# A place for side work inside each projection of a two-layer decoder trunk, and other costs in its plan

## The chip, the cores and the metric

The kernel runs on one core of a Trainium2 chip. The metric is the device time of one execution in microseconds (us); the kernel before takes 852.53 us (median of three runs, 852.04 to 853.74). PE is the tensor engine (PEld its weight loads), DVE the vector engine, ACT the scalar engine, POOL the GpSimd engine, SP the engine that issues the weight DMAs.

## What is computed

Two layers over 256 tokens of width 1024 in float32. One input projection feeds three branches: sliding-window attention with sinks (8 heads of 64, window 128), a gated short convolution, and block-selected attention (which for 256 tokens is plain causal attention of 8 heads). Gates merge them, an output projection, residual and LayerNorm follow, then a SwiGLU network of hidden width 2816, residual and LayerNorm. Cut to its frame, the reference is:

```python
for l in range(2):
    proj = x @ w_in[l]                       # q,k,v | conv h,b,c | q,k,v | three gates
    y_a = sliding_window_attention(a_q, a_k, a_v, sinks[l])
    y_b = b_b * causal_conv3(b_c * b_h, conv_w[l])
    y_c = causal_attention(c_q, c_k, c_v)    # ALiBi, as in y_a
    mix = (sigmoid(g_a) * (y_a @ w_a) + sigmoid(g_b) * (y_b @ w_b) + sigmoid(g_c) * (y_c @ w_c)) @ w_out[l]
    x = layer_norm(ALPHA * x + mix)
    x = layer_norm(ALPHA * x + (silu(x @ w_gate) * (x @ w_up)) @ w_down)
```

## The kernel before

Every large product is computed as three float32r products: a tensor is split into a high part (a copy into float32r) and a low part (the difference), and high x high, high x low and low x high are added in PSUM. Weights come in pieces of 128 x 2048 (139 of them after the first), each loaded by SP as a megabyte. ACT copies the high parts of a piece (`wh`, L180) and DVE subtracts the low parts (`wl`, L181), in two chunks of 1024 columns each. The activations (`xx`, both parts) stay in SBUF.

The main stream of PE is `whole` (L371): it takes one piece and makes two accumulators `acc` of 128 x 256, each from 8 depth steps of three matmuls (`trio`), so 24 matmuls an accumulator. `half_pair` (tile `hp`), `branch` (`br`), `merge` (`gc`) and `project` (`pr`) are the same for other shapes.

Side work of PE is attention, one pair of heads a round, 8 rounds a layer (4 of the sliding window, then 4 of the other, called MoBA in the code): `scores` (tile `s`, 6 matmuls), a softmax on DVE and ACT (tile `prob`), `turned` (6 transposes of `prob` into `tp`, which ACT copies to `pt`), and `mixed` (tile `yp`, probabilities times values, which ACT and DVE split into `y`). The transposes of LayerNorm's output (`xtok`) and of `qh` and `gh` are side work too. POOL computes the convolution's taps (L721 to L724, five products and sums an accumulator); DVE multiplies their sum by an accumulator (L277 `t<-t,acc`) and splits it.

The order on every engine is written when the program is built, by a planner, `Plan`. It keeps a clock of PE (`T.pe`, advanced by `pe_time` for each matmul) and a time at which ACT (A), DVE (V) and POOL (G) are free. A task is a list of operations, each with an engine and a cost. `run` issues, in order of their planned start, all operations that can start before PE's clock; `finish` advances PE's clock to a task's end where PE must wait for it. `dve(n)` and `act(n)` give the cost of an operation on n columns. The function `tick` is where side work gets its place on PE: it runs the planner, and issues a waiting piece only when, by the planned clock, its inputs are there (`settled`), or when it is forced. A tick stands after each accumulator of 24 matmuls. The engines execute their lists in order, with semaphores for the true dependences: if the plan is wrong, the work is still right, but an engine waits.

Of the kernel before, what the change touches and what calls it, by code (L numbers as in the profile page):

```python
# [20 lines left out]
KD = D // P  # L21
# [82 lines left out]
def pe_time(cols):  # L104
    return cols / 2400 + 0.0067


def dve(n):
    return "V", 0.07 + n * 0.00104


def act(n):
    return "A", 0.07 + n * 0.00083


@with_exitstack
def trunk(ctx: ExitStack, tc: tile.TileContext, x, first, w, sinks, conv, ln, out):
# [9 lines left out]
    T = Plan()  # L127
# [88 lines left out]
    def settled(task):  # L216
        return task is None or task.done and task.ready <= T.pe

    def tick(force=False):
        while True:  # L220
            T.run()
            go = [e for e in waiting if force or settled(e[0])]
            if go:
                waiting.remove(go[0])
                if go[0][0] is not None:
                    T.finish(go[0][0])
                go[0][1]()
            elif rounds and not rounds[0].tasks and rounds[0].known(force):
                rounds[0].prepare()
            elif rounds and rounds[0].tasks and not busy[0] and (force or all(settled(t) for t in rounds[0].tasks)):  # L230
                busy[0] += 1
                r = rounds.pop(0)
                T.finish(*r.tasks)
                r.scores()
                if not force:
                    return
            else:
                return
# [3 lines left out]
    def bank(shape, tag, name):  # L242

        t = ps.tile(shape, FT, tag=tag, name=name)
        if len(banks[tag]) >= 4:
            for task in banks[tag].pop(0):
                T.finish(task)
        banks[tag].append([])
        return t, banks[tag][-1]
# [75 lines left out]
    for k in steps:  # L325
        xk_, wk = both[:, k, 0:S], both[:, k, S:].rearrange("p k (m c) -> p m k c", m=2)
        n = (k.stop - k.start) * S
# [38 lines left out]
    def trio(acc, wh, wl, src, first, last):  # L366
        mm(acc, wh, src[:, 0, :], first, False)
        mm(acc, wh, src[:, 1, :], False, False)
        mm(acc, wl, src[:, 0, :], False, last)

    def whole(done, by_step=False):  # L371
        j = take()
        wh, wl = duo(j)
        accs = [bank([P, S], "mm", "acc") for m in range(2)]
        order = [(m, k) for m in range(2) for k in range(KD)]
        if by_step:
            order.sort(key=lambda mk: mk[1])
        for m, k in order:
            acc, users = accs[m]
            trio(acc, wh[:, m, k, :], wl[:, m, k, :], xk[k], k == 0, k == KD - 1)  # L380
            if k == KD - 1:
                if m:
                    drop(j)
                done(m, acc, users)
                tick()
# [36 lines left out]
    def attend(q, k, new_k, xq, xk, v, vsel, far, slopes, sink, dst, when):  # L422
        los = [slice(a * HD, (a + 1) * HD) for a in range(2)]
        pr, pts, tasks = [], [], []

        def soft(a, st, t, s):
            def top():
                nc.vector.tensor_reduce(st[:, 0:1], t[:, 0, :], axis=AX.X, op=OP.max)
                nc.vector.tensor_reduce(st[:, 1:2], t[:, 1:3, :], axis=AX.XY, op=OP.max)
                if sink is not None:  # L430
                    nc.vector.tensor_scalar(st[:, 2:4], st[:, 0:2], sink[1][a], -0.125, op0=OP.max, op1=OP.mult)
                else:
                    nc.vector.tensor_scalar_mul(st[:, 2:4], st[:, 0:2], -0.125)  # L433

            def power():
                nc.scalar.activation(t[:, 0, :], t[:, 0, :], AF.Exp, bias=st[:, 2:3], scale=0.125,  # L436
                                     accum_out=st[:, 4:5])
                nc.scalar.activation(t[:, 1:3, :], t[:, 1:3, :], AF.Exp, bias=st[:, 3:4], scale=0.125,
                                     accum_out=st[:, 5:6])
                if sink is not None:  # L440
                    nc.scalar.activation(st[:, 6:8], st[:, 2:4], AF.Exp, bias=sink[0][a], scale=1.0)

            def scale():
                if sink is not None:
                    nc.vector.tensor_add(st[:, 4:6], st[:, 4:6], st[:, 6:8])
                nc.vector.reciprocal(st[:, 6:8], st[:, 4:6])
                nc.vector.tensor_scalar_mul(t[:, 0, :], t[:, 0, :], st[:, 6:7])
                nc.vector.tensor_scalar_mul(t[:, 1:3, :], t[:, 1:3, :], st[:, 7:8])

            return [  # L450
                dve(384) + (lambda: nc.vector.scalar_tensor_tensor(t, far, -8.0 * slopes[a], s[:, 0:3, :],  # L451
                                                                   op0=OP.mult, op1=OP.add),),
                dve(P) + (lambda: nc.vector.tensor_add(t[:, 0, :], t[:, 0, :], s[:, 3, :]),),
                ("V", 0.75, top), ("A", 1.1, power), ("V", 0.9, scale)]

        def scores():
            ss = [bank([P, 4, P], "o", "s") for a in range(2)]
            for a in range(2):
                s = ss[a][0]
                mm(s[:, 1:3, :], xq[:, a, P:S], xk[:, a, 0, :], True, False)  # L460
                mm(s[:, 1:3, :], xq[:, a, P:S], xk[:, a, 1, :], False, True)
                mm(s[:, 0::3, :], xq[:, a, 0:P], xk[:, a, :, 0:P], True, True)
            for a in range(2):
                st = work.tile([P, 8], FT, name="st", bufs=4)
                pr.append(work.tile([P, 3, P], FT, tag="prob", name="prob", bufs=4))
                tasks.append(after(ss[a][1], soft(a, st, pr[a], ss[a][0])))
            later(tasks[-1], turned)

        def turned():
            T.finish(*tasks)  # L470
            for a in range(2):
                tp, users = turn(lambda i: pr[a][:, i, :], 3)
                pts.append(work.tile([P, 3, P], FT, name="pt"))
                tasks.append(after(users, copy(pts[a], tp, 384)))
            later(tasks[-1], mixed)

        def mixed():
            T.finish(*tasks)
            yp, users = bank([P, S], "o", "yp")
            for a in range(2):  # L480
                nc.tensor.matmul(yp[los[a], :], v[:, 0, vsel[a]], pts[a][:, 0:2, :], start=True, stop=False)  # L481
            for a in range(2):
                nc.tensor.matmul(yp[los[a], P:S], v[:, 1, vsel[a]], pts[a][:, 2, :], start=False, stop=True)
            T.pe += pe_time(4 * 384)
            at["y"].append(after(users, halve(dst, yp, S), due=8.0))
            busy[0] -= 1

        rounds.append(Round(when, q, k, new_k, xq, xk, scores))
# [450 lines left out]
```

## Time and profile before

| | |
|---|---|
| median of 3 runs | 852.53 us (852.04 to 853.74) |
| profiled execution: time, span | 849.59 us, 847.8 us |
| PE busy | 831.9 us, 98% |
| DVE busy | 583.0 us, 69% |
| ACT busy | 455.1 us, 54% |
| POOL busy | 51.8 us, 6% |
| mean granted TensorE clock | 0.998 |

A busy time is the union of an engine's instructions. Matmuls overlap in their pipeline: one of 128 x 256 is shown with some 280 ns, while the next starts some 115 ns later. So PE's rate is read from starts, and its loss from gaps and from starts that come late. An engine's idle time is put down to the instruction that ended it (the releaser).

### The profile page before, as it was taken

How to read it: one execution, taken by the hardware profiler on the slowest of the kernel's cores; microseconds unless marked ns; L12 is line 12 of the kernel's file. 1: busy time of each engine (PE TensorE's matmuls, PEld its weight loads, DVE VectorE, ACT ScalarE, POOL GpSimd, SP SyncE). 2: the span in 40 equal slices, each digit the busy share in tenths (PEclk: the TensorE clock that was granted, in tenths of full speed). 3: DMA queues.
4: the chain of work that ended last, by engine and by line, in shares of the span. 5: the costliest groups of instructions: out<-in, count | busy, mean ns of one | idle time of the engine just before them, and what ended most of it. 6: DMA issues, size and time to landing. Idle time of an engine off the chain costs nothing.

```text
span 847.8 us, 15535 instructions
## 1 busy us (share of the span) xinstructions
PE 831.9 (98%) x6388; PEld 791.2 (93%) x6388; DVE 583.0 (69%) x978; ACT 455.1 (54%) x809; POOL 51.8 (6%) x81
## 2 busy tenths in 40 slices
PE   8999999999999999999999999999999999999996
PEld 7989989999899999988899899999998999999885
DVE  5678888677967566545657898886688566566435
ACT  6767587746525445434347857786573345444320
POOL 2003400000100000000000034000000000000000
PEclk9999999999999999999999999999999999999999
DMA  9753525555655555556337352545657365555511
GB/s 316 282 211 137 199 101 198 164 186 199 248 199 200 181 172 194 199 191 235 121 106 255 138 197 101 177 150 174 226 188 281 124 225 195 196 171 183 197 50 49
DMA packets 23462, 155.15 MB, mean 183 GB/s; under 512 B 2624, under 2 KB 2912, under 8 KB 5984
## 3 DMA queue, kind: packets, MB, share of 16 engines
q1 hardware_dynamic: 21888, 149.17, 50.1%
q0 software_dynamic: 1216, 4.22, 1.5%
q8 instruction: 50, 0.82, 0.4%
q10 hardware_dynamic: 288, 0.79, 0.3%
q14 instruction: 20, 0.16, 0.1%
HBM read 153.11 MB, written 1.05 MB: 182 GB/s over the span
## 4 chain that ended last, share of the span: by engine, by line
PE 83%; DVE 6%; ACT 4%; DMA 3%; POOL 2%; issue 1%; SPq 0%; POOLq 0%; DVEq 0%; ACTq 0%
PE acc L252 38%; PE pr L252 18%; PE hp L252 8%; PE br L252 8%; PE gc L252 5%; PE cv L252 3%; DMA raw<-w 2%; PE tp L265 2%; DVE wl L181 1%; ACT wh L180 1%; DMA gb<-ln 1%; PE s L252 1%; PE yp L481 1%; POOL hh L723 1%; DVE prob L451 1%
## 5 line engine op out<-in xcount | busy, mean ns | idle before, releaser
L252 PE MATMUL acc<-xx,wh 128*128 128x256 f32 x2304 | 405.1, 280 | 2.4 <-ACT wh L270 2.4
L181 DVE TENSOR_TENSOR wl<-raw,wh 128x1024 fp32r<-128x1024 f32 x266 | 321.5, 1228 | 116.0 <-ACT wh L180 114.9
L180 ACT ACTIVATE wh<-raw 128x1024 fp32r<-128x1024 f32 x266 | 273.4, 1054 | 185.5 <-PE acc L252 81.9
L252 PEld LDWEIGHTS acc<-xx,wh 128*128 128x128 f32 x2304 | 351.0, 189 | 3.4 <-ACT wh L270 2.9
L252 PE MATMUL acc<-xx,wl 128*128 128x256 f32 x1152 | 321.7, 279 | 0.3 <-DVE wl L271 0.2
L252 PEld LDWEIGHTS acc<-xx,wl 128*128 128x128 f32 x1152 | 216.4, 188 | 0.8 <-DVE wl L271 0.7
L252 PE MATMUL hp<-wh,xx 128*128 128x256 f32 x384 | 70.5, 281 | 0.0
L277 DVE TENSOR_TENSOR g<-g,acc 128x256 f32<-128x256 f32 x72 | 30.0, 416 | 58.7 <-PE acc L252 58.7
L252 PE MATMUL br<-y,wh 128*128 128x256 f32 x384 | 66.7, 278 | 0.0
L252 PE MATMUL pr<-wh,hidA 128*128 128x512 f32 (+1 forms) x216 | 60.7, 366 | 0.0
L252 PEld LDWEIGHTS hp<-wh,xx 128*128 128x128 f32 x384 | 59.5, 188 | 0.0
L252 PEld LDWEIGHTS br<-y,wh 128*128 128x128 f32 x384 | 58.3, 189 | 0.0
L252 PE MATMUL hp<-wl,xx 128*128 128x256 f32 x192 | 53.5, 279 | 0.0
L252 PE MATMUL br<-y,wl 128*128 128x256 f32 x192 | 53.5, 278 | 0.0
L252 PEld LDWEIGHTS pr<-wh,hidA 128*128 128x128 f32 x216 | 39.1, 189 | 6.7
L252 PE MATMUL gc<-xx,wh 128*128 128x256 f32 x256 | 44.5, 278 | 0.0
L252 PE MATMUL pr<-wh,hidB 128*128 128x512 f32 (+1 forms) x144 | 41.8, 366 | 0.0
L252 PE MATMUL pr<-wl,hidA 128*128 128x512 f32 (+1 forms) x108 | 39.6, 366 | 0.0
L252 PEld LDWEIGHTS gc<-xx,wh 128*128 128x128 f32 x256 | 38.9, 189 | 0.0
L436 ACT ACTIVATE prob<-prob,st 128x128 f32<-128x128 f32 x32 | 12.6, 395 | 45.3 <-DVE st L433 23.3
L252 PEld LDWEIGHTS hp<-wl,xx 128*128 128x128 f32 x192 | 36.1, 188 | 0.0
L252 PEld LDWEIGHTS br<-y,wl 128*128 128x128 f32 x192 | 36.0, 188 | 0.0
(133 smaller groups left out, 976.9 us busy)
## 6 DMA issues: line engine op xcount, KB each, us to landing
raw<-w SPq DMA_DIRECT2D x136, 1024.0 KB, 4.9
gb<-ln POOLq DMA_DIRECT2D x8, 512.0 KB, 5.9
raw<-w SPq DMA_DIRECT2D x6, 512.0 KB, 10.4
first<-first SPq DMA_DIRECT2D x2, 512.0 KB, 7.6
xtok<-x SPq DMA_DIRECT2D x2, 512.0 KB, 6.2
out<-xtok SPq DMA_DIRECT2D x3, 256.0 KB, 2.0
first<-first ACTq DMA_DIRECT2D x1, 512.0 KB, 7.7
first<-first ACTq DMA_DIRECT2D x1, 256.0 KB, 4.2
```

The costliest lines, as they stand in the source:

```text
L180: return [act(n) + (lambda: nc.scalar.activation(wh[:, s], raw[j][:, s], AF.Copy),), dve(n) + (lambda: nc.vector.tensor_sub(wl[:, s], raw[ ...
L181: dve(n) + (lambda: nc.vector.tensor_sub(wl[:, s], raw[j][:, s], wh[:, s].bitcast(FT)),)]
L252: nc.tensor.matmul(acc, a, b, start=start, stop=stop)
L265: nc.tensor.transpose(tp[:, i, :], src(i), ident)
L277: return [dve(n) + (lambda: nc.vector.tensor_mul(dst, a, b),)]
L436: nc.scalar.activation(t[:, 0, :], t[:, 0, :], AF.Exp, bias=st[:, 2:3], scale=0.125, accum_out=st[:, 4:5])
L451: dve(384) + (lambda: nc.vector.scalar_tensor_tensor(t, far, -8.0 * slopes[a], s[:, 0:3, :], op0=OP.mult, op1=OP.add),),
L481: nc.tensor.matmul(yp[los[a], :], v[:, 0, vsel[a]], pts[a][:, 0:2, :], start=True, stop=False)
L723: nc.gpsimd.tensor_mul(other, up[:, i, n:S + n], tap[n])
```

## The change

A tick also stands in the middle of each accumulator's 24 matmuls, after 12 (depth step 4 of 8), except where the first piece goes by depth step (`by_step`). And the plan's costs are larger: an operation of n columns on DVE is planned with 0.15 + 0.00106 n us in place of 0.07 + 0.00104 n, on ACT with 0.18 + 0.00085 n in place of 0.07 + 0.00083 n; the three softmax steps with 0.95, 1.5 and 1.1 us in place of 0.75, 1.1 and 0.9; and PE's clock gets 0.1 us more for `scores` and 0.25 us more for `mixed`. No operation is added or taken away: only the order changes.

```diff
 def dve(n):
-    return "V", 0.07 + n * 0.00104
+    return "V", 0.15 + n * 0.00106
 
 
 def act(n):
-    return "A", 0.07 + n * 0.00083
+    return "A", 0.18 + n * 0.00085
...
             trio(acc, wh[:, m, k, :], wl[:, m, k, :], xk[k], k == 0, k == KD - 1)
+            if k == KD // 2 - 1 and not by_step:
+                tick()
             if k == KD - 1:
...
-                ("V", 0.75, top), ("A", 1.1, power), ("V", 0.9, scale)]
+                ("V", 0.95, top), ("A", 1.5, power), ("V", 1.1, scale)]
...
             ss = [bank([P, 4, P], "o", "s") for a in range(2)]
+            T.pe += 0.1
...
-            T.pe += pe_time(4 * 384)
+            T.pe += pe_time(4 * 384) + 0.25
```

What this does to the order is shown at two places. The first is on PE, in the second sliding-window round of layer 0: the last matmuls of an accumulator between the transposes of `prob` and the products `yp`, with the rows of before marked - and those of the changed kernel + (lines 481 and 483 have become 484 and 486).

```order
-L252 MATMUL acc<-xx,wh 128x256 x2
-L252 MATMUL acc<-xx,wl 128x256
-L252 MATMUL acc<-xx,wh 128x256 x2
-L252 MATMUL acc<-xx,wl 128x256
-L252 MATMUL acc<-xx,wh 128x256 x2
-L252 MATMUL acc<-xx,wl 128x256
-L252 MATMUL acc<-xx,wh 128x256 x2
-L252 MATMUL acc<-xx,wl 128x256
-L481 MATMUL yp<-pt,mix 64x256 x2
-L483 MATMUL yp<-pt,mix 64x128 x2
+L484 MATMUL yp<-pt,mix 64x256 x2
+L486 MATMUL yp<-pt,mix 64x128 x2
```

Twelve matmuls leave the space between the transposes and `yp` and come behind the next scores: 12 are left of 24. The same happens in 5 rounds of each layer (the second, third, fifth, seventh and eighth); in the first it was 12 matmuls of twice the width before and is still, in the fourth and sixth it stays 24.

The second place is the fifth round, the first of MoBA, in layer 0. On ACT before, from the softmax's last powers (L436, L438) to the copies `pt`:

```order
L436 ACTIVATE prob,st<-prob,st 128x128
L438 ACTIVATE prob,st<-prob,st 128x256
L270 ACTIVATE y<-t_1223 128x256
L270 ACTIVATE xa<-mix 64x256 x4
L274 ACTIVATE gs<-acc 128x256
L180 ACTIVATE wh<-raw 128x1024
L274 ACTIVATE xa<-mix 64x256 x2
L180 ACTIVATE wh<-raw 128x1024
L274 ACTIVATE pt<-tp 128x384 x2
```

On ACT in the changed kernel, the same stretch (the powers are now L438 and L440):

```order
L438 ACTIVATE prob,st<-prob,st 128x128
L440 ACTIVATE prob,st<-prob,st 128x256
L270 ACTIVATE y<-t_1186 128x256
L274 ACTIVATE xa<-mix 64x256
L180 ACTIVATE wh<-raw 128x1024
L274 ACTIVATE gs<-acc 128x256
L180 ACTIVATE wh<-raw 128x1024
L274 ACTIVATE xa<-mix 64x256
L274 ACTIVATE pt<-tp 128x384
L274 ACTIVATE gs<-acc 128x256
L270 ACTIVATE y<-t_1238 128x256
L274 ACTIVATE pt<-tp 128x384
```

Four of the six `xa` copies (the next round's queries and keys) have gone ahead of the powers, and two other operations now stand between the two `pt` copies. On DVE before, the same round, from the convolution's product `mix<-acc,hh` to the scores' first operation `prob<-far_c,s`; `t_1181` is the sum of taps that POOL makes from that product:

```order
L277 TENSOR_TENSOR mix<-acc,hh 128x256
L181 TENSOR_TENSOR wl<-raw,wh 128x1024
L277 TENSOR_TENSOR mix<-acc,hh 128x256
L181 TENSOR_TENSOR wl<-raw,wh 128x1024 x3
L277 TENSOR_TENSOR t_1181<-t_1181,acc 128x256
L271 TENSOR_TENSOR y<-yp,y 128x256
L271 TENSOR_TENSOR y<-t_1181,y 128x256
L451 SCALAR_TENSOR_TENSOR prob<-far_c,s 128x384 x2
```

On DVE in the changed kernel, where that sum is called `t_1186`:

```order
L181 TENSOR_TENSOR wl<-raw,wh 128x1024 x2
L277 TENSOR_TENSOR mix<-acc,hh 128x256
L181 TENSOR_TENSOR wl<-raw,wh 128x1024
L453 SCALAR_TENSOR_TENSOR prob<-far_c,s 128x384 x2
L455 TENSOR_TENSOR prob<-prob,s 128x128 x2
L430 TENSOR_REDUCE st<-prob 128x1
L431 TENSOR_REDUCE st<-prob 128x1
L435 TENSOR_SCALAR st<-st 128x2
L430 TENSOR_REDUCE st<-prob 128x1
L431 TENSOR_REDUCE st<-prob 128x1
L435 TENSOR_SCALAR st<-st 128x2
L277 TENSOR_TENSOR t_1186<-t_1186,acc 128x256
```

The product with the taps' sum, which stood ahead of the scores' operations, stands behind the maxima of both heads.

## Rows read from the trace of the kernel before

**Rows 1.** The page's first part: busy us, share of the span, instructions.

```profile
PE 831.9 (98%) x6388; PEld 791.2 (93%) x6388; DVE 583.0 (69%) x978; ACT 455.1 (54%) x809; POOL 51.8 (6%) x81
```

**Rows 2.** What PE waited for: us in total, times, longest.

```profile
PE yp L481 <- ACT pt L274: 3.1, 3, 1.5
PE acc L252 <- ACT wh L270: 2.4, 2, 1.5
...
PE tp L265 <- ACT qh L274: 0.8, 1, 0.8
PE tp L265 <- DVE xtok L509: 0.8, 1, 0.8
```

**Rows 3.** Timeline of PE around four visits to yp: start, us, instructions.

```profile
127.20 0.28 PE L252 MATMUL acc<-xx,wl 128*128 128x256 f32 x1
128.21 0.38 PE L252 MATMUL s<-xa 128*128 128x256 f32 x1
...
97.74 0.28 PE L252 MATMUL acc<-xx,wl 128*128 128x256 f32 x1
99.23 0.39 PE L252 MATMUL s<-xa 128*128 128x256 f32 x1
...
111.72 0.28 PE L252 MATMUL acc<-xx,wl 128*128 128x256 f32 x1
114.63 0.38 PE L252 MATMUL s<-xa 128*128 128x256 f32 x1
...
514.88 0.28 PE L252 MATMUL acc<-xx,wl 128*128 128x256 f32 x1
516.50 0.39 PE L252 MATMUL s<-xa 128*128 128x256 f32 x1
```

**Rows 4.** Timeline of ACT in the fifth round of layer 0, idle before in brackets.

```profile
106.03 0.40 ACT L436 ACTIVATE prob<-prob,st 128x128 f32<-128x128 f32 x1 [2.67 <-DVE st L433]
...
108.11 1.45 ACT L270 ACTIVATE xa<-mix 64x256 fp32r<-64x256 f32 x4
...
112.93 0.85 ACT L274 ACTIVATE pt<-tp 128x384 f32<-128x384 f32 x2
```

**Rows 5.** Timelines of POOL and DVE, the same round.

```profile
95.38 1.46 POOL L721 TENSOR_TENSOR t<-mix,cw 128x256 f32<-128x256 f32 x1 [14.87 <-DVE mix L277]
...
101.71 0.74 POOL L724 TENSOR_TENSOR t<-t,hh 128x256 f32<-128x256 f32 x1
102.41 0.61 POOL L721 TENSOR_TENSOR t<-mix,cw 128x256 f32<-128x256 f32 x1
...
96.71 4.45 DVE L181 TENSOR_TENSOR wl<-raw,wh 128x1024 fp32r<-128x1024 f32 x3
102.48 0.42 DVE L277 TENSOR_TENSOR t<-t,acc 128x256 f32<-128x256 f32 x1 [1.32 <-POOL t L724]
```

**Rows 6.** Groups of the page: busy us, mean ns, idle before, releaser.

```profile
L181 DVE TENSOR_TENSOR wl<-raw,wh 128x1024 fp32r<-128x1024 f32 x266 | 321.5, 1228 | 116.0 <-ACT wh L180 114.9
L180 ACT ACTIVATE wh<-raw 128x1024 fp32r<-128x1024 f32 x266 | 273.4, 1054 | 185.5 <-PE acc L252 81.9
```

**Rows 7.** Timelines of PE and DVE at layer 1's first LayerNorm.

```profile
645.25 0.66 PE L265 MATMUL tp<-ident,xtok 128*128 128x128 f32 x4 [0.77 <-DVE xtok L509]
...
644.44 1.41 DVE L509 SCALAR_TENSOR_TENSOR xtok<-xtok,mv,gb 128x512 f32<-128x512 f32 x2 [0.83 <-DMA gb<-ln]
```

**Rows 8.** Timelines of PE and ACT in the seventh round of layer 0.

```profile
137.20 0.82 PE L265 MATMUL tp<-ident,prob 128*128 128x128 f32 x6
140.68 0.65 PE L481 MATMUL yp<-pt,mix 128*64 128x256 f32 x4
...
139.74 0.85 ACT L274 ACTIVATE pt<-tp 128x384 f32<-128x384 f32 x2
```

**Rows 9.** Timelines of PE and ACT behind layer 0's first LayerNorm.

```profile
245.53 1.03 PE L265 MATMUL tp<-ident,xtok 128*128 128x128 f32 x8
...
246.16 1.09 ACT L270 ACTIVATE xx<-tp 128x512 fp32r<-128x512 f32 x2 [2.88 <-PE tp L265]
```

## The prediction

> **What bounds the kernel now.** I read the page's busy times first, then the list of what PE waited for, then PE's timeline at those waits, and last ACT, DVE and POOL at the same times, to see what made PE's input late. PE is busy for 98% of the span [rows 1]. Weights never hold it up behind the start: apart from the 2.4 us at the start for the first copies, every wait of PE in its list is for a small piece of side work [rows 2]. So the change, which takes no matmul away, can win only what PE loses at side work, a few us of 850, and can lose as much by new waits.
>
> How much is lost is read from starts, since a busy PE hides half of it. In an undisturbed round the last matmul ahead of `yp` starts at 127.20 and the next scores at 128.21, 1.01 us later [rows 3]. In the fourth round of layer 0 the same stretch takes 99.23 - 97.74 = 1.49 us, in the fifth 114.63 - 111.72 = 2.91, and in the fourth of layer 1 516.50 - 514.88 = 1.62 [rows 3]. The fifth of layer 1 is taken as equal to that of layer 0 (the three idle gaps sum to 3.1 us with a longest of 1.5 [rows 2], so one more of about 1.5 is there). Lost: 0.48 + 1.90 + 0.61 + 1.90 = 4.9 us.
>
> Why the fifth round: POOL starts the convolution's taps at 95.38 and ends the first sum at 102.45, 7.07 us for five operations; the next accumulator's first tap takes 0.61 us where this one took 1.46 beside DVE's weight subtractions, and these three took 4.45 us [rows 5]. The plan counts 4.0 us for the five. DVE's list has the product with that sum ahead of the scores, and DVE waits 1.32 us there [rows 5]; so the powers start only at 106.03 after ACT had idled 2.67 us, six `xa` copies and two splits follow, and the `pt` copies start at 112.93, when `yp` was due at about 111.8 [rows 3, 4].
>
> **The change, part by part.**
>
> *The costs.* A weight chunk of 1024 was planned with 1.13 us on DVE and 0.92 on ACT, and is now planned with 1.24 and 1.05; the trace has 1.228 and 1.054 [rows 6]. The planned clock of DVE and ACT therefore no longer runs ahead of the engines', while PE's (256 columns: 0.113 us) is still no slower than PE, so a piece that the plan calls settled should mostly be there. What the new list makes of the fifth round: behind the product `mix<-acc,hh` PE has 12 matmuls, 6 transposes, 24 matmuls, `yp` and the scores. At 0.115 us a matmul (3.48 us for the 6 transposes and 24 matmuls of [rows 8]) that is 1.4 + 3.5 + 1.0 + 0.7 = 6.6 us to the scores' end. DVE then runs ten operations, 2 x 0.56 + 2 x 0.29 + 2 x 0.95 = 3.6 us by the plan's new costs, before it comes to the product with the taps' sum, at about 10 us. The taps, started 0.6 us behind the accumulator's end and again beside three subtractions, need 7.1, so they are done at about 7.7 us: DVE doesn't wait, and the powers are ready some 3 us earlier than before. Four `xa` copies have also gone ahead of the powers. I take the fifth rounds' waits as gone, and the fourth's too (24 matmuls remain there, and fewer splits stand ahead): 4.9 us won.
>
> The two `pt` copies of the fifth round are now parted by a `gs` and a `y` copy: 0.48 + 0.38 + 0.42 + 0.48 less 0.3 of overlap is 1.5 to 1.8 us from the first copy's start to the second's end. The transposes allow a first copy about 0.5 us after they start (four of them let the `xx` copy start after 246.16 - 245.53 = 0.63 us [rows 9]), and the second product of `yp` is due 2.4 us after it: a margin of 0.1 to 0.4 us, nothing more.
>
> *The place in the middle.* In 5 rounds of each layer `yp` now stands 12 matmuls nearer to its transposes: 140.68 - 137.20 = 3.48 us becomes 3.48 - 12 x 0.115 = 2.1 us [rows 8]. The copy then has to start within 2.1 - 0.48 = 1.6 us. In the seventh round it started after 139.74 - 137.20 = 2.54 us [rows 8], 0.9 us too late, if ACT's list were as before. In the new list a split and several `xa` copies (1.05 and 0.4 us each) fewer stand ahead of it. Bounds: 0 below, and 0.9 us in the seventh rounds of both layers, with as much in one round more, 2.4 us together; I take 0.5, near the lower end, because each of these lists is shorter by more than 0.9 us.
>
> *LayerNorm.* The first transposes of `xtok` in layer 1 waited 0.77 us [rows 7], for a LayerNorm operation that itself waited 0.83 us for the DMA of `gb` [rows 7]. Both slices now come together 6 matmuls of 512 later, 6 x 0.23 = 1.4 us, which covers the wait: 0.8 won. The other half's second slice goes the other way, in both layers: it comes 24 matmuls later, at the very end of the work that needs only the first half. Behind it stand 2 transposes and the 12 matmuls that read the first slice, about 0.7 + 1.4 + 0.2 = 2.3 us to the first use of the second slice's low part. The copy starts 0.63 us after its transposes, and copy and subtraction take 0.6 + 0.7 us, so it is there after 1.9 to 2.0 us [rows 9]. Cost 0, from 0 to 0.7 us a layer should a split of 1.05 us stand in the way on ACT, which its list doesn't show.
>
> *What stays.* ACT's list is the same as before to the copy that the first `qh` transposes wait for, so that 0.8 us stays, with the start's 2.4 [rows 2]. The weights' loads keep their order on SP, POOL's list too, and the last LayerNorm keeps its order on every engine.
>
> **Sum**, against the profiled execution's own 849.6 us: -4.9 - 0.8 + 0.5 = -5.2, so 844.4. That execution is 2.9 us below the median of the runs, 852.53, and no row shows why; the change is therefore taken from the median: 847.3 us. The likeliest case alone, with its unknown costs (2.4 for 0.5, 1.4 for 0), reaches from 846.8 to 850.6.
>
> **A rule against it.** The trace has a tap of 1.46 us beside weight subtractions and one of 0.61 without [rows 5]. The Trainium skill, page "SBUF — State Buffer", section "Who interferes with whom", says that a DVE instruction with two inputs in SBUF contends with a GpSimd instruction that reads SBUF, by an exclusive lock: the loser is blocked, it doesn't share. By that rule three subtractions of 1.22 us would lengthen five taps of about 3.4 us (0.61 to 0.74 each undisturbed) to 7.1, and the trace's 7.07 agrees. Planned costs taken from the trace can't see this, and the taps' 4.0 is not among the numbers changed; by this rule alone the fifth rounds would keep their waits, which is the first rival.
>
> **Rivals.**
>
> *The taps still decide the fifth rounds.* `yp` stands as far behind its scores as before (96 matmuls, 84 and 12 now, 72 and 24 then). If the product with the taps' sum still holds up DVE, the two waits of 1.9 us come back: a gain of 5.2 - 3.8 = 1.4 us, 851.1 us. For it: the plan's unchanged 4.0 against 7.07, and DVE's wait of 1.32 [rows 5]. Against it: the product stands behind the maxima now, 2 us after the taps should be done. With it I count any case in which the waits only move to other rounds. Chance 0.16.
>
> *The shortened rounds wait: slower.* In ten rounds `yp` needs its copy within 1.6 us of the transposes. If ACT comes as late in all of them as in the seventh of before, each costs 0.9 us: +9.0, with 5.7 won elsewhere, so +3.3, 855.8 us. It turns to a loss when more than six of the ten are that late. For it: the copies of the seventh round, 0.9 us too late by today's list [rows 8]; ACT has 1.05-us splits that can't be interrupted. Against it: the tick only places what the plan calls settled, and ACT idles 185 us ahead of its splits alone [rows 6], so its list has room. Chance 0.10.
>
> **How the numbers follow.** Forecast 0.74, the taps' rival 0.16, the slower one 0.10. A measurement of this kernel can tell about 0.2%, 1.7 us, from no change: the forecast's range lies wholly beyond that on the fast side, the first rival's 1.4 within it, the other's 3.3 beyond it on the slow side. The range of 8 in 10 goes from 845.4 (all 5.7 won, and 1.4 us for runs that spread by 1.7) to 852.4, which takes in the first rival and leaves out the slower one and about as much below.
>
> **What would show it.** Right: PE's waits for `pt` all but gone (3.1 us before), the fifth rounds' stretch from the last matmul to the scores back at about 1.0 us, no wait for `xtok`, the wait for `qh` still there; the powers of the fifth round about 5 us behind their scores. Wrong: a wait of PE for `pt` in the second, third, seventh or eighth rounds, of DVE for POOL's sum ahead of the powers, or of `hp` for `xx` at the second slice. A time above 851 us would say that the planned clock isn't what made PE wait.

## The result, and the profile after

The changed kernel takes 846.41 us (median of four runs, 844.5 to 849.0), the kernel before in the same session 852.28 (851.86 to 853.74): a ratio of 0.9931, 95% interval 0.9912 to 0.995. Forecast were 847.3 us and "faster". Run again beside other kernels, the changed one took 846.91 us (0.9931, 0.9906 to 0.9955) and the one before 852.13. So the gain is 5.2 to 5.9 us.

The first profile of the changed kernel is its slowest run: 849.0 us, span 847.2. What PE waited for in it (us in total, times, longest), to set beside [rows 2]:

```profile
PE acc L252 <- ACT wh L270: 4.5, 2, 3.0
PE spin L322 <- DVE xtok L319: 1.1, 1, 1.1
PE tp L265 <- DVE xtok L512: 0.6, 1, 0.6
...
```

The 3.1 us for `pt` are gone, and so are the 0.8 for `qh`; the wait for `xtok` is nearly as long as it was, and the start has become worse. The start is chance of this execution: the first operands landed late (ACT idled 3.12 us for them), and TensorE's granted clock fell behind PE's 2.98 us wait, as the windows of PE show (the stretch: its length, us busy, instructions, granted clock, DMA share, GB/s; a clock of 0.50 is the lower of its two levels, 1.2 in place of 2.4 GHz, so 0.81 and 0.62 say that PE had it for 3.4 us in all):

```profile
7.00:10.00 3.00, 0.87 (x8) 1.00 0.99 262
10.00:13.00 3.00, 1.93 (x9) 0.81 1.04 422
13.00:16.00 3.00, 3.00 (x19) 0.62 1.02 416
```

The second profile of the same kernel (846.48 us, span 844.7) has the first scores at 44.31 us where the first had 46.54, with the same list of instructions. The account below is therefore made from the second profiles of both kernels (before: 850.74 us, span 849.0).

PE around the fourth and fifth rounds' `yp` of layer 0, in the seventh round, and at layer 1's LayerNorm (first profile of the changed kernel; start, us), which answers to [rows 3, 7, 8]:

```profile
98.66 0.28 PE L252 MATMUL acc<-xx,wl 128*128 128x256 f32 x1
...
99.67 0.98 PE L252 MATMUL s<-xa 128*128 128x256 f32 x6
...
110.03 0.82 PE L265 MATMUL tp<-ident,prob 128*128 128x128 f32 x6
...
111.94 0.28 PE L252 MATMUL acc<-xx,wl 128*128 128x256 f32 x1
112.15 1.09 PE L484 MATMUL yp<-pt,mix 128*64 128x256 f32 x3
...
113.60 0.98 PE L252 MATMUL s<-xa 128*128 128x256 f32 x6
...
135.88 0.82 PE L265 MATMUL tp<-ident,prob 128*128 128x128 f32 x6
138.01 0.65 PE L484 MATMUL yp<-pt,mix 128*64 128x256 f32 x4
...
646.01 1.32 PE L265 MATMUL tp<-ident,xtok 128*128 128x128 f32 x8 [0.59 <-DVE xtok L512]
```

In the fourth round the last matmul now leads to the scores in 1.01 us (1.49 before), in the fifth in 1.66 (2.91 before). The shortened seventh round has `yp` 2.13 us behind its transposes, with no wait. ACT, DVE and POOL in the fifth round, three fences, answer to [rows 4, 5]; the last row of ACT is in the seventh round, the first of DVE in the fourth, the last of DVE at layer 1's LayerNorm:

```profile
104.14 0.40 ACT L438 ACTIVATE prob<-prob,st 128x128 f32<-128x128 f32 x1 [0.44 <-DVE st L435]
...
110.61 0.49 ACT L274 ACTIVATE pt<-tp 128x384 f32<-128x384 f32 x1 [0.85 <-PE tp L265]
111.00 0.38 ACT L274 ACTIVATE gs<-acc 128x256 f32<-128x256 f32 x1
111.96 0.42 ACT L270 ACTIVATE y<-t 128x256 fp32r<-128x256 f32 x1 [0.58 <-DVE t L277]
112.28 0.47 ACT L274 ACTIVATE pt<-tp 128x384 f32<-128x384 f32 x1
...
136.47 0.87 ACT L274 ACTIVATE pt<-tp 128x384 f32<-128x384 f32 x2 [0.28 <-PE tp L265]
```

```profile
88.53 0.42 DVE L277 TENSOR_TENSOR t<-t,acc 128x256 f32<-128x256 f32 x1 [1.31 <-POOL t L727]
...
105.16 0.41 DVE L277 TENSOR_TENSOR t<-t,acc 128x256 f32<-128x256 f32 x1
...
110.04 1.22 DVE L181 TENSOR_TENSOR wl<-raw,wh 128x1024 fp32r<-128x1024 f32 x1
...
111.52 0.41 DVE L277 TENSOR_TENSOR t<-t,acc 128x256 f32<-128x256 f32 x1
...
645.20 1.41 DVE L512 SCALAR_TENSOR_TENSOR xtok<-xtok,mv,gb 128x512 f32<-128x512 f32 x2 [2.02 <-DMA gb<-ln]
```

```profile
97.88 1.46 POOL L724 TENSOR_TENSOR t<-mix,cw 128x256 f32<-128x256 f32 x1 [9.39 <-ACT pt L274]
...
100.97 1.60 POOL L727 TENSOR_TENSOR t<-t,hh 128x256 f32<-128x256 f32 x1
102.65 0.61 POOL L726 TENSOR_TENSOR hh<-mix,cw 128x256 f32<-128x256 f32 x1
103.34 0.74 POOL L727 TENSOR_TENSOR t<-t,hh 128x256 f32<-128x256 f32 x1
```

The taps are done at 104.08 and the product with their sum starts at 105.16 without waiting for them: the powers stand 4.5 us behind the scores instead of 6.8 (106.03 - 99.23 [rows 3, 4]). What is left of the fifth round's wait is the second `pt` copy: behind the `y` copy, which waits 0.58 us for DVE's second product, which stands behind a subtraction of 1.22 us.

DVE's wait for POOL's sum has not gone, it has moved to the fourth round: 1.31 us ahead of the operations on that round's scores (88.53), where it was 1.32 in the fifth [rows 5], and 2.6 us in both layers together before and after. The fourth round's powers start 6.4 us behind its scores, nearly as late as the fifth's did before (6.8). PE loses nothing by it, because `yp` of the fourth round now stands 108 matmuls behind its scores where it stood 96, 12 x 0.113 = 1.36 us more: the copies end 1.1 us before it is due.

Worked out from the starts on PE, the stretches of some kernels, in us, layer 0 and layer 1 (attention: first scores to first `br`; output: from the first `pr` behind merge to the first `hp`; SwiGLU: from there to the next `pr`; the kernels whose first scores come 12 matmuls early have 12 more in attention, and 12 x 0.1133 = 1.36 us are taken off there). The second profiles of both kernels stand first:

| kernel | attention | branch and merge | output, LayerNorm | SwiGLU | span |
|---|---|---|---|---|---|
| before | 112.06, 112.20 | 56.53, 56.53 | 23.25, 23.20 | 126.13, 126.14 | 849.0 |
| changed | 109.94, 109.94 | 56.53, 56.53 | 22.70, 23.45 | 126.00, 126.00 | 844.7 |
| costs alone | 115.22, 115.34 | 54.78, 55.58 | 22.68, 22.97 | 125.95, 125.95 | 852.4 |
| place alone | 111.26, 111.38 | 56.53, 56.53 | 23.44, 23.57 | 126.14, 126.14 | 850.2 |
| copies, gb halves | 111.32, 111.38 | 56.53, 56.53 | 24.25, 24.24 | 126.00, 126.00 | 850.9 |
| place in gates only | 108.96, 108.96 | 56.63, 56.63 | 22.70, 22.70 | 125.95, 125.95 | 843.4 |
| the same, with turns | 108.96, 108.96 | 55.25, 55.25 | 22.67, 22.67 | 122.88, 122.88 | 834.6 |

Before to changed: -2.1 and -2.3 in attention, -0.6 and +0.3 at the LayerNorms, some -0.5 in the rest, and +0.9 up to the first scores (44.74, against 44.31 + 1.36): -4.3, the difference of the spans. The medians' 5.2 to 5.9 are about a microsecond more; what comes before the first scores varies by more than that (43.91 to 46.91 us in seven profiles with one and the same start).

### The profile page after: what moved, and what is told of

The parts are those of the page before. It is cut to its first block, busy times and chain, and to the rows that moved or that the text cites. A ratio compares the mean times of both kernels' runs of the same rounds, so it can differ in the third digit from the quotient of the medians.

```text
span 847.2 us, 15506 instructions
## 1 busy us (share of the span) xinstructions
PE 833.2 (98%) x6388; PEld 793.3 (94%) x6388; DVE 582.7 (69%) x978; ACT 456.0 (54%) x809; POOL 56.8 (7%) x81
## 4 chain that ended last, share of the span: by engine, by line
PE 96%; DMA 2%; DVE 1%; ACT 0%; issue 0%; POOLq 0%; POOL 0%; SPq 0%; DVEq 0%
PE acc L252 47%; PE pr L252 17%; PE hp L252 9%; PE br L252 8%; PE gc L252 5%; PE cv L252 3%; PE tp L265 2%; PE s L252 2%; DMA gb<-ln 1%; PE yp L484 1%; DMA first<-first 1%; PE yp L486 0%; DVE xtok L512 0%; DVE wA L181 0%; POOLq L938 0%
## 5 line engine op out<-in xcount | busy, mean ns | idle before, releaser
L252 PE MATMUL acc<-xx,wh 128*128 128x256 f32 x2304 | 405.9, 280 | 4.5 <-ACT wh L270 4.5
L252 PEld LDWEIGHTS acc<-xx,wh 128*128 128x128 f32 x2304 | 351.2, 189 | 5.6 <-ACT wh L270 5.0
L252 PE MATMUL acc<-xx,wl 128*128 128x256 f32 x1152 | 322.1, 280 | 0.2 <-DVE wl L271 0.2
L252 PEld LDWEIGHTS acc<-xx,wl 128*128 128x128 f32 x1152 | 219.3, 190 | 0.6 <-DVE wl L271 0.4
L252 PE MATMUL hp<-wh,xx 128*128 128x256 f32 x384 | 70.4, 281 | 0.0
L252 PE MATMUL br<-y,wh 128*128 128x256 f32 x384 | 67.9, 281 | 0.0
L252 PE MATMUL pr<-wh,hidA 128*128 128x512 f32 (+1 forms) x216 | 60.7, 366 | 0.0
L252 PEld LDWEIGHTS hp<-wh,xx 128*128 128x128 f32 x384 | 59.5, 188 | 0.0
L252 PEld LDWEIGHTS br<-y,wh 128*128 128x128 f32 x384 | 58.9, 190 | 0.0
L252 PE MATMUL br<-y,wl 128*128 128x256 f32 x192 | 54.0, 281 | 0.0
L252 PE MATMUL hp<-wl,xx 128*128 128x256 f32 x192 | 53.5, 279 | 0.0
L252 PE MATMUL gc<-xx,wh 128*128 128x256 f32 x256 | 45.3, 281 | 0.0
L252 PEld LDWEIGHTS pr<-wh,hidA 128*128 128x128 f32 x216 | 39.1, 189 | 6.6
L252 PE MATMUL pr<-wh,hidB 128*128 128x512 f32 (+1 forms) x144 | 41.8, 366 | 0.0
L252 PE MATMUL pr<-wl,hidA 128*128 128x512 f32 (+1 forms) x108 | 39.5, 366 | 0.0
L252 PEld LDWEIGHTS gc<-xx,wh 128*128 128x128 f32 x256 | 39.3, 190 | 0.0
L252 PEld LDWEIGHTS hp<-wl,xx 128*128 128x128 f32 x192 | 36.1, 188 | 0.0
L252 PEld LDWEIGHTS br<-y,wl 128*128 128x128 f32 x192 | 36.0, 188 | 0.0
L252 PE MATMUL gc<-xx,wl 128*128 128x256 f32 x128 | 36.0, 281 | 0.0
## 6 DMA issues: line engine op xcount, KB each, us to landing
raw<-w SPq DMA_DIRECT2D x6, 512.0 KB, 11.3
```

What stands on the lines that cost most here:

```text
L252: nc.tensor.matmul(acc, a, b, start=start, stop=stop)
```

## The experiments

**The costs alone, and the place alone.** Each half of the change by itself: `costs_only` is the changed kernel without the tick in the middle, `tick_only` the kernel before with it.

```diff
-            if k == KD // 2 - 1 and not by_step:
-                tick()
```

> The new costs alone, no place in the middle of an accumulator. Theory A (the planned clock that ran ahead of ACT and DVE made PE wait): the fourth and fifth rounds' waits go as in the changed kernel, since the scores now stand 96 matmuls ahead of their transposes there; that is -4.9 us. But the eighth rounds are pushed to the end of the accumulators, with no matmul between the transposes and yp, so PE must wait there for both pt copies: the transposes take 0.7 us, the second copy ends about 2.1 us behind their start, 1.4 us a layer, +2.8. Expected 852.3 - 4.9 + 2.8 = 850.2 us (849 to 851.5). Theory B (it is the place in the middle that wins): no gain, 852.3 or above, with the fifth round's wait of PE for pt still there.

> The place in the middle alone, with the old costs. Theory A: the plan now calls pieces settled even further ahead of the engines. In the fifth round the transposes stand 60 matmuls (6.9 us) behind the scores, and ACT has two splits, two xa copies and a y copy (3.4 us) between the powers and the pt copies: PE waits for pt 1 to 2 us in each fifth round and some tenths in other rounds with only 12 matmuls. Expected 853 us (851.5 to 856), with PE's waits for pt or prob at 3 us or more in all. Theory B (the place alone wins): 846 to 849 us, with no such waits.

Measured: the costs alone 854.67 us, slower (1.0025, 1.0009 to 1.0041); the place alone 850.69 (0.9973, 0.9956 to 0.999). Neither half makes the gain: against 852.46 us beside them, the costs alone lose 2.2 us and the place alone wins 1.8. PE's timeline with the costs alone, at the eighth round of layer 0:

```profile
153.25 0.28 PE L252 MATMUL acc<-xx,wl 128*128 128x256 f32 x1
156.43 0.61 PE L265 MATMUL tp<-ident,prob 128*128 128x128 f32 x3 [2.90 <-DVE prob L447]
158.22 0.86 PE L265 MATMUL tp<-ident,prob 128*128 128x128 f32 x3 [1.18 <-DVE prob L447]
159.01 1.40 PE L482 MATMUL yp<-pt,mix 128*64 128x256 f32 x3
...
161.19 0.75 PE L252 MATMUL br<-y,wh 128*128 128x256 f32 x2
```

The fourth and fifth rounds are as theory A had them: `yp` 3.48 us behind its transposes in both, on time. But three rounds now have 96 matmuls between scores and transposes in place of 72, the eighth is pushed to where the projections run out, and only 24 stand behind its scores: PE waits 4.1 us for `prob` and goes straight from the transposes to `yp`. The expectation had counted the wait for the copies (1.4 us a layer) and not that for `prob`. The windows around the wait show what follows it:

```profile
153.30:158.20 4.90, 0.84 (x6) 1.00 0.38 161
158.20:161.80 3.60, 3.58 (x14) 0.53 0.80 280
...
```

With 0.84 of 4.90 us busy, PE is granted 0.53 of its clock in the next 3.6 us (the lower level, 0.50, for 3.4 us of them; in layer 1, behind the same wait, for 6.8 us). This belongs to the program: the mean granted clock is 0.989 to 0.994 in all its twelve runs, 0.995 or more in those of the kernel before beside them. In attention the costs alone lose 3.2 and 3.1 us by the table; that the whole is not worse is in part owed to the shorter spacing of matmuls in branch and merge (54.78 and 55.58 us for 56.53), of which more below. The place alone has the opposite fault. Its fifth round still waits, with the transposes 60 matmuls behind the scores:

```profile
107.16 0.81 PE L483 MATMUL yp<-pt,mix 128*64 128x256 f32 x3 [0.49 <-ACT pt L274]
```

Its 850.69 us lies between the ranges of the two theories: it loses less than theory A expected, since the product with the taps' sum stands behind the scores there too. So the mechanism of the prediction (a clock that runs ahead makes PE wait) is borne out in the rounds, and its account of the two edits is not: the larger costs need the place in the middle, or the last rounds don't fit.

**The same two kernels again**, to see what belongs to the program.

> The changed kernel once more. 846.4 us as before (845 to 848). What its first profile showed that the change can't have made tells itself here: if the late start (first transfer about 2 us later, 3.4 us at half the granted clock) and the slower spacing of the matmuls in branch and merge of layer 1 (117.8 ns instead of 113.3) were chance of that execution, they are gone or elsewhere in this profile and its span is 2 to 4 us shorter; if the program makes them, they are in the same place. The wait of the second pt copy in the fifth rounds (0.65 us each, ACT behind DVE's product with the taps' sum) and LayerNorm's wait for gb (0.6 us) belong to the program and should be there again.

> The kernel before once more. 852.3 us (851.9 to 853.7). If its first profile (849.6 us, 2.7 under the median) was a lucky one, this profile is at 851.5 to 853, and the difference lies in the spacing of the matmuls (more of them at 117.8 ns) and not in the waits for side work, which should be the same to 0.2 us each: 3.1 us for pt, 0.8 for qh, 0.8 for xtok. If the spacing belongs to the program, the same stretches show the same spacing as before.

Measured: 846.91 and 852.13 us. The late start and the half clock were chance: they aren't in the second profile of the changed kernel, where the slow matmuls, some 0.21 us apart, are the first twelve alone. The 3.1 us for `pt` before, and the fifth rounds' second copy after, are there to 0.02 us. The wait for `qh` isn't there in either second profile: it was chance too. So was something else: in layer 1 of the first profile before, branch took 32.64 us, in the second 33.92, with no wait in either (windows of L252 on PE, first profile, then second):

```profile
574.94:607.58 32.64, 32.64 (x291) 1.00 0.54 184
```

```profile
574.45:608.37 33.92, 33.92 (x290) 1.00 0.51 177
```

The same 288 matmuls start every 113.3 ns in the one and every 117.8 in the other, at a granted clock of 1.00 in both. With merge that is 2.1 us, most of the 2.9 by which that profile lay below its median.

**What is left of the fifth round, and gb.** Both transposes are issued first, then both copies; and gb is loaded in halves.

```diff
+            tps = [turn(lambda i: pr[a][:, i, :], 3) for a in range(2)]
-                tasks.append(after(users, copy(pts[a], tp, 384)))
+                tasks.append(after(users, copy(pts[a], tp, 384), due=-50.0))
...
+        for e in (slice(0, 512), slice(512, D)):
+            nc.gpsimd.dma_start(g[:, e], ln[l, i, e].partition_broadcast(P))
+            nc.gpsimd.dma_start(b[:, e], ln[l, i + 1, e].partition_broadcast(P))
```

> Two small edits at separate places. (1) Both transposes of a round are issued before their two pt copies, and the copies come first in the plan: they stand side by side on ACT in every round, with a gs and a split more ahead of them in the fifth. Theory A (the fifth rounds' rest is the y copy between the pt copies, that waits for DVE's product): the second pt copy of the fifth round ends about 2.0 us behind its transposes' start instead of 2.7, PE's second yp product no longer comes late, -0.65 us in each layer. Rival: the split ahead of the copies takes the gain back, the first copy ends after 2.1 us and the stretch stays as long. (2) gb, the scale and shift of the LayerNorm, comes in halves of 512 columns, the first halves of both first. If layer 1's wait for xtok is the transfer of gb (DVE waits 1.7 to 2.0 us for it), it lands some 4 us earlier and that wait is gone, -0.3 to -0.6 us; if not, it stays. Together 846.9 - 1.3 - 0.4 = 845.2 us (844.5 to 847).

Measured: 851.74 us, the gain gone. The fifth round's second copy now ends 2.41 us behind the transposes in place of 2.74, half of what was expected. But the lists behind it have changed too. PE's waits, then ACT, then DVE ahead of the sixth round's operations on the scores, which PE started at 112.08:

```profile
PE tp L265 <- DVE xtok L512: 2.2, 4, 0.6
PE tp L265 <- DVE prob L449: 2.1, 4, 0.6
```

```profile
115.12 1.06 ACT L180 ACTIVATE wh<-raw 128x1024 fp32r<-128x1024 f32 x1 [3.59 <-DMA raw<-w]
```

```profile
116.22 1.23 DVE L181 TENSOR_TENSOR wl<-raw,wh 128x1024 fp32r<-128x1024 f32 x1 [0.61 <-ACT wh L180]
117.36 1.01 DVE L453 SCALAR_TENSOR_TENSOR prob<-far_c,s 128x384 f32<-128x384 f32 x2
```

A subtraction now stands ahead of the scores' first operation; it waits for ACT's split, and that for its weights. So DVE starts on the scores 5.3 us behind them, where it was 3.1 in the changed kernel, `prob` is late, and the round loses more than the fifth won. And gb in halves is worse: its four transfers of 256 KB land 9.5 and 9.6 us behind their issue (medians, layers 0 and 1), where two of 512 KB land after 7.2 and 9.7 in the changed kernel's second profile. The last of the four is there 13.4 us behind the first issue in both layers, the last of the two after 10.0 and 11.9. DVE's list has the second slice's product with the scale ahead of the first slice's sum with the shift, so it waits 1.9 and 2.0 us for the second half of the scale, the third load to land, and comes late for both slices in both layers. That the wait for `xtok` is gb's is shown by its releaser; that halves would shorten it was wrong.

**The taps with a larger cost.**

```diff
-                made[4 + m] = after([], [("G", 4.0, taps)], needs=[made[2 + m]])
+                made[4 + m] = after([], [("G", 7.1, taps)], needs=[made[2 + m]])
```

> One number in the changed kernel's plan: POOL's five tap operations are planned with 7.1 us (as the trace has them in the fifth round) in place of 4.0. Theory A (with the new costs the taps no longer decide anything but the y copy between the fifth round's pt copies): at most the second pt copy moves, 846 to 847.5 us. Rival (the taps' wrong cost is what is left of the fifth round's loss, 0.65 us a layer): 845.6 us, with the second yp product on time. What speaks against any gain: the product with the second sum still stands late, and a y copy still stands between the two pt copies; and the fourth round's place is now 12 matmuls behind its transposes where ACT's pt copies started 1.5 us behind them, so 0 to 0.5 us may be lost there.

Measured: 850.04 us (0.9991, 0.9977 to 1.0005). The fifth round's copies are on time, and the waits are in the fourth (for `pt`) and the sixth (for `prob`):

```profile
PE tp L265 <- DVE prob L449: 1.1, 2, 0.6
PE yp L484 <- ACT pt L274: 0.9, 2, 0.5
```

In attention that is 1.7 us a layer more than the changed kernel has. Both theories missed that. Nor is 7.1 the taps' cost: in the changed kernel the four sums of a layer take 3.9, 6.3, 6.2 and 3.6 us, with this plan 3.9, 6.3, 4.4 and 6.1. One number for all four, taken from the slowest of the kernel before, made a worse order.

**Where the place in the middle earns its part.** It is offered in the gate accumulators only.

```diff
-            if k == KD // 2 - 1 and not by_step:
+            if k == KD // 2 - 1 and middle:
...
-                whole(done)
+                whole(done, middle=True)
```

> The new costs, with the place in the middle only in the sixteen gate accumulators of each layer (the last projection stretch of a layer's attention). Theory A (with the new costs the place in the middle is worth the 5.8 us between 852.5 + 2.2 and 846.9 because it gives the last rounds a place before the projections run out; the rounds it shortens elsewhere give and cost nothing): the eighth round keeps 84 matmuls behind its scores and 12 behind its transposes, PE's 7.9 us of waits for prob are gone, and the time is that of the changed kernel plus up to 1.5 us for the fifth round, whose yp now comes 84 matmuls behind its scores in place of 96: 847 to 848.5 us. Rival (the short distance between transposes and yp wins time in every round, by bringing the next scores forward): about half of the gain is left, 850 to 851 us.

Measured: 844.32 us (0.9922, 0.99 to 0.9944), below the range of either theory. It is 2.6 us below the changed kernel's second median, but in another session: against the kernel before beside each the ratios are 0.9922 and 0.9931 and their intervals overlap, so the times alone don't show it to be the faster of the two. The stretches of the table do, for the profiled executions: 1.0 us less attention in each layer, 0.75 less at layer 1's LayerNorm. No wait for `pt`, `prob` or the LayerNorm's `xtok` is left (`spin` is at the start):

```profile
PE acc L252 <- ACT wh L270: 2.9, 3, 1.6
PE spin L322 <- DVE xtok L319: 1.1, 1, 1.1
PE acc L252 <- DVE wl L271: 0.4, 2, 0.2
```

The eighth round has its place (84 matmuls, then 12), and the fifth round's copies end 1.47 us behind the transposes, although its scores stand only 72 matmuls ahead. So the places outside the gates win nothing here; with them the fifth round lost 0.7 us a layer.

**The two spacings.** First one matmul or six, of the shape of scores, were added ahead of branch and in the SwiGLU stretch (`mm` on operands from `xx`, the result unused).

> The changed kernel with work added: six more matmuls of the shape of scores (operands from xx, the result is not used), once a layer ahead of the branch products and once at the third of the eighteen pairs of accumulators of the SwiGLU stretch. They cost 0.7 us each, 2.8 us in all. Theory A (the matmuls have two spacings, about 113.3 and 117.8 ns, at one granted clock; the spacing is set at a visit to side work, a visit of scores sets the short one, and it holds to the next visit): 480 matmuls of branch and merge and 768 of the SwiGLU accumulators go from 117.8 to 113.3 ns in each layer, -2.2 and -3.5 us, less 1.4: -4.3 us a layer, 846.9 - 8.6 = 838.3 us. If only branch and merge take it: 846.9 - 4.4 + 2.8 = 845.3. Theory B (the spacing belongs to the stretch, by its operands and its weight traffic): 849.7 us, and the spacing stays at 117.8 ns behind both visits.

> As the kernel with six added matmuls at each of the two places, but with one matmul at each: cost 0.12 us each, 0.5 us in all. Theory A, if any change of tiles between two kinds of matmul is enough to set the short spacing: 846.9 - 11.4 + 0.5 = 836 us. If the visit must be longer, or end in the strided pair that the scores end in: 847.4 us and no change of spacing. Theory B: 847.4 us.

Measured: 849.04 and 846.69 us, and 117.8 ns behind both: no change of spacing. Matmuls of scores' shape alone don't do what a round does. Then one kernel with sixteen kinds of visit, one ahead of each pair of accumulators.

> The changed kernel with a different short visit of extra PE work (results not used) ahead of each of sixteen pairs of accumulators of the SwiGLU stretch, in both layers: 1, 2, 3, 4, 6 and 8 transposes, products of the shape of yp alone and with scores behind them, six and three of the shape of scores in two accumulators or one, and matmuls of 512 and 128 columns, of 64 rows, and with another moving tile. And 3 transposes ahead of layer 0's branch products, 6 ahead of layer 1's. Only the spacing of the 48 matmuls behind each visit is read; the total is some 20 us longer. Theory A (the spacing is set by how a visit ends): it changes behind some kinds and the same kinds in both layers; by the rounds, 6 transposes and yp with scores should set 113.3 ns, 2 transposes and yp alone 117.8. Theory B (the spacing belongs to the tiles of the stretch): all at 117.8 ns, whatever stands ahead; then 864 matmuls a layer can't be had faster in this way.

Measured: 867.38 us, and the answer in the windows behind 1, 2, 3, 4 and 6 transposes, 48 matmuls each (the counts take in what overlaps an edge):

```profile
267.72:273.46 5.74, 5.74 (x50) 1.00 0.67 213
273.60:279.33 5.73, 5.73 (x49) 1.00 0.47 164
279.58:285.12 5.54, 5.54 (x48) 1.00 0.50 179
285.48:291.22 5.74, 5.74 (x48) 1.00 0.51 188
291.79:297.33 5.54, 5.54 (x48) 1.00 0.46 149
```

Behind 3, 5, 6 and 8 transposes, `yp` with scores, two matmuls of 512 columns, three of 128 or of 64 rows, or six with another moving tile, the spacing is 113.3 ns; behind 1, 2 and 4, `yp` alone, three or six of scores' shape, and 6 transposes with `yp` and scores, it is 117.8: in both layers alike. That speaks against theory B. It bears out of theory A that the kind of visit goes with the spacing, and not its reason, how a visit ends: `yp` with six of scores' shape, those six alone, and 6 transposes with `yp` and the six all end alike, and only the first is followed by 113.3 ns. Ahead of branch, 3 transposes left the long spacing and 6 set the short one. That is used in a version with work added to go faster: on top of the place in the gates, 3 transposes of `ident` in the SwiGLU stretch, and 6 at branch, first straight behind `yp`, then behind the first branch accumulator:

```diff
+            if f == 6:
+                turn(lambda i: ident, 3)
...
+                    if b == 0 and i == 1:
+                        for _ in range(2):
+                            turn(lambda i: ident, 3)
```

> The kernel with the middle place in the gate accumulators alone, and two visits a layer of transposes whose result is not used: 6 ahead of the branch products (0.55 us) and 3 ahead of the SwiGLU stretch's third pair of accumulators (0.25 us). Theory A (a visit sets the matmul spacing by how it ends, and it holds until the next visit): as behind 6 and 3 transposes in the run of visits, the 480 matmuls of branch and merge and the 768 behind f = 6 go from 117.8 to 113.3 ns: -2.1 and -3.4 us for 0.8, -4.7 a layer, 844.3 - 9.4 = 834.9 us (833 to 837). Theory B (the short spacing holds for some 50 matmuls and falls back): under 1 us won by it, 844 to 846 us. A third way: the transposes ahead of branch come here straight behind yp and not behind an accumulator, and leave the long spacing there, 844.3 + 1.1 - 6.3 = 839.1 us.

> As the kernel with 6 transposes ahead of the branch products, but these 6 stand behind the first branch accumulator (12 matmuls) instead of straight behind yp. Theory A (6 transposes set the short spacing when they stand behind an accumulator, as in layer 1 of the run of visits): 276 branch and 192 merge matmuls a layer go to 113.3 ns, -2.1 us each, 839.4 - 4.2 = 835.2 us (834.5 to 836.5). If the branch products keep the long spacing behind 6 transposes whatever stands ahead: 839.4 us, as before.

Measured: 839.42 us (0.9858, 0.9842 to 0.9874), the third way: straight behind `yp` branch stays long. Then 836.05 us (0.9803, 0.978 to 0.9826), with branch, merge and SwiGLU of layer 0 in these windows; the SwiGLU stretch of before, 840 matmuls, under them from its second profile:

```profile
158.14:189.53 31.39, 31.39 (x277) 1.00 0.51 173
189.53:211.29 21.76, 21.76 (x195) 1.00 0.53 188
269.70:356.84 87.14, 87.14 (x769) 1.00 0.56 193
```

```profile
263.69:362.71 99.02, 99.02 (x842) 1.00 0.56 192
```

87.14 / 768 = 113.5 ns against 99.02 / 840 = 117.9. The short spacing held for 768 matmuls, to the next visit. This version beats both kernels: it is 15.6 us below the one before, and its interval lies wholly below the changed kernel's (0.9906 to 0.9955).

## Why the prediction was right, and where it was not

- *The sum* (-5.2): -4.3 between the second profiles, -5.2 to -5.9 between the medians. That it fits so well is in part luck: the waits and LayerNorm gave 0.5 us less than forecast each, the shortened rounds cost 0.5 less, and some 0.5 came in stretches for which the prediction has no term.
- *The waits at `yp`* (-4.9): -2.1 and -2.3 measured in attention, so 4.4. Of it 3.6 us are the four places named: the fourth rounds' waits went whole, each fifth round kept 0.65 of 1.90. Another 0.5 are in the sixth and seventh rounds, whose stretches from the last matmul to the scores, 1.12 to 1.15 us in the second profile before, are 1.01. The step that was mis-sized is the margin of the second `pt` copy: the prediction saw that a `gs` and a `y` copy part the two copies and added up their durations, but the `y` copy also waits for DVE's product, 0.58 us, and the margin of 0.1 to 0.4 was gone.
- *The shortened rounds* (+0.5): 0. In all but the fifth the copies end 1.46 us behind the transposes, 0.66 ahead of `yp` (in the seventh round from 135.88 to 137.34). The slower rival asked for more than six of ten that come late; there was one in each layer.
- *The taps' rival*: its time didn't come, but its wait is still there. POOL's operations are as slow as before where they run beside DVE's subtractions (1.46 and 1.60 us, 0.61 and 0.74 without), and the fifth round's five, planned with 4.0 us, take 6.2. By the rule in the Trainium skill, page "SBUF — State Buffer", section "Who interferes with whom" (a DVE instruction with two inputs in SBUF contends with a GpSimd instruction that reads SBUF, for an exclusive lock), that was to be expected, and the trace agrees. In the fifth round the product's new place behind the maxima makes it harmless, as the prediction argued. In the fourth DVE waits for POOL's sum ahead of the powers, 1.31 us, which the prediction named as a sign that it is wrong; there it is the 12 matmuls more of cover that keep PE from waiting, and the prediction has no such term.
- *LayerNorm* (-0.8): about -0.3. The first transposes of layer 1 came later, as predicted, and DVE's wait for gb grew from 0.83 to 2.02 us in the first profile (1.7 in the second). The prediction took the transfer's time as given, and the later transposes to cover the wait; but the second of the two loads landed 11.6 and 11.3 us behind its issue, where it took 9.6 and 9.0 in the two profiles of the kernel before (layer 1). What made it longer is open. The second slice cost 0, as predicted.
- *What stays*: the wait for `qh` didn't, but it isn't in the second profile of before either; and the first scores came 12 matmuls earlier, which only moves work.
- *The attribution*: the weakest step. The prediction gave the whole gain to the costs and only a cost to the place in the middle. Alone, the costs lose 2.2 us. The order of the changed kernel, from which the gain was read, was right; the reason for it was half right.
- *The median as the base*: sound. That the first profile of before lay 2.9 us below it had a reason that no row of it names: for 2.1 of it, the spacing in layer 1's branch and merge.

## What to carry to other kernels

A planner's costs and its places belong together: costs that are true but larger push work back, and if the last piece then has no cover left, the engine loses there more than it won; so read the end of each list first. A number that is right for one operation of a kind can make a worse order, and each edit to a plan moves everything behind it: measure whole orders. And read the spacing of an engine's starts, not only its gaps: 98% busy hid 4% of PE's rate over nearly half of the program.

## What the runs showed that was not expected

- Matmuls of 128 x 256 with a new stationary tile each have two spacings, 113.3 and 117.8 ns, at a granted clock of 1.00. One holds until the next visit of other work (here up to 768 or 840 matmuls), and which follows goes with what the visit is and what stands ahead of it: 6 transposes were followed by the short one behind an accumulator, by the long one straight behind `yp`. Sixteen kinds behaved alike in two layers. Why is open: the visits stood in one order only, so the spacing ahead of a visit isn't told apart from its kind, and I found no start of DVE, ACT or POOL that the changes have in common.
- In one stretch the spacing was chance: layer 1's branch in the kernel before, 113.3 ns in one execution and 117.8 in the other.
- Behind 4.9 us with 0.84 busy, the granted clock was 0.53 for 3.6 us.
- The first scores stand up to 3.0 us apart between runs of one order. In the changed kernel's two profiles, 2.2 us apart, the slower start has ACT idle 3.12 us for the first operands and the lower clock behind it.
- The same five operations of POOL take from 3.5 to 7.1 us: in the fifth round 1.46 to 1.60 us each beside DVE's subtractions, 0.61 to 0.74 without.
